# Hybrid decoder trunk on one core: the FFN's weight sums come from accumulating DMAs in DRAM instead of VectorE

## The chip, the cores and the metric

The kernel runs on one core of one Trainium2 chip. The metric is the device time of one execution in microseconds (us). The engines are TensorE (PE), VectorE (DVE), ScalarE (ACT), GpSimd (POOL) and SyncE (SP); DMAs are issued from the queues of SP, ACT or POOL and run on the 16 DMA engines of the core.

## The reference

The model has two layers of width 1024 over 1024 tokens, in float32. Layer 0 mixes by Mamba-2 SSD heads and gMLP heads, layer 1 by a Conformer convolution and HGRN2 heads. Each mixer is followed by a squared-ReLU MLP (FFN), and one RMSNorm ends the model. The part that the change touches is the first half of the MLP:

```python
for layer in range(DEPTH):                      # DEPTH = 2
    ...                                         # mixer: x = x + y
    h = rmsnorm(x, ffn_norm_g[layer])           # x: 1024 x 1024
    x = x + jnp.square(jax.nn.relu(h @ ffn_w1[layer])) @ ffn_w2[layer]   # w1: 1024 x 4096
return rmsnorm(x, final_norm_g)
```

The weights are drawn anew for each set of inputs, so every sum of weights has to be formed on the chip.

## The kernel before

Activations are kept with channels on the 128 partitions and tokens along the free axis, as 8 tiles of 128 x 1024. Every large product is computed in float32 by three matmuls with operands in fp32r: `split` (lines 97 to 100) makes a high part by a cast on ACT and the remainder by a subtraction on DVE, and the matmuls take high x high, high x low and low x high.

The FFN input, `ffn_in`, is one level of Winograd's form of Strassen's product. The 1024 x 1024 input is cut into quadrants (channels in two halves, tokens in two halves). `wino_ops` forms the seven operands of the activation side (B11, B21, T1, T2, T3, B22, T4) while the output projection of the mixer ends, each as a tile whose first 512 columns hold the high part and whose last 512 hold the low part. The 4096 hidden channels are 32 blocks of 128; one *unit* takes two of them, `w1[2u]` and `w1[2u+1]`, each a 128 x 1024 tile in which the columns 0 to 511 are the first half of the input channels and 512 to 1023 the second. There are 16 units in a layer. A unit needs seven products, and a product is 4 x 3 matmuls of 512 columns (lines 330 to 332).

The weight side of the seven products comes from the generator `weights`. It loads two tiles for a unit (`wraw`, three buffers, from SP's queue), forms four sums and differences of quadrants on DVE (`comb`, line 345), and splits all seven operands one by one into tiles of their own: high part in the columns 0 to 511, low part in 512 to 1023. Eight such tiles exist. `nextw` keeps the emission of operands four ahead of the products. The first two products of the first three units (`nhead`) need only plain quadrants and are emitted ahead of the rest; their weight tiles are loaded a second time when the units go on.

After each product the running sums in PSUM are copied by ACT (`snap`), added on DVE, and passed through ReLU and a square on ACT; the hidden tiles go to DRAM from ACT's queue and come back for the FFN output.

The program is written in order, and a scheduler places the instructions of each engine by priority and by its own estimate of when operands are ready; `high_priority` moves a block ahead. `issue_after(ins)` makes the instructions that its block traces on the engine of `ins` queue behind `ins`. Each engine, and each DMA queue, then runs strictly in its own order. SP's queue carries nearly all loads. POOL's carries no DMA in the kernel before, only 12 memsets besides the constants: two on `rmask` at the start (line 1185) and the others for layer 1.

At the start, `gmlp` loads two weight blocks of `wv` in halves of 520 KB and the input x in segments of 256 columns, in turn, on SP's queue, and the first products run as these land. In the SSD part, `prep` reloads a broadcast of the cumulative sums (`A<-acs_d`, 512 KB) for every chunk.

Of the kernel before, what the change touches and what calls it, by code (L numbers as in the profile page):

```python
# [1 line left out]

# [4 lines left out]
F32 = mybir.dt.float32  # L7
# [3 lines left out]
AF = mybir.ActivationFunctionType  # L11
ALU = mybir.AluOpType
# [3 lines left out]
P = 128  # L16
D = 1024
T = 1024
HALF = 512
# [20 lines left out]
HP = 500  # L40
# [4 lines left out]
def R(ap):  # L45
    return ap.bitcast(F32R)
# [10 lines left out]
class Trunk:  # L57
# [178 lines left out]
                self.nc.scalar.activation(rs, rs, AF.Square)  # L236


    def wino_start(self, X, g, spill):
        return dict(X=X, g=g, acc=None, spill=spill, ops={}, late=[])  # L240

    def wino_ops(self, st, r, k):

        nc, X, tt = self.nc, st["X"], self.nc.vector.tensor_tensor
        n = r.stop - r.start

        def op(name, src, q):
            if (name, k) not in st["ops"]:
                st["ops"][name, k] = self.slot(name)
            t = st["ops"][name, k]  # L250
            self.split(src, t[:, q], t[:, HALF + q.start:HALF + q.stop])

        y, z = X[k][:, r], X[k + 4][:, r]
        for i, x in ((k, y), (k + 4, z)):
            nc.scalar.activation(x, x, AF.Copy, scale=self.v(st["g"], i))
        if r.stop <= HALF:
            op("B11", y, r)
            op("B21", z, r)
            return
        q = slice(r.start - HALF, r.stop - HALF)  # L260
        b11, b21 = X[k][:, q], X[k + 4][:, q]
        t2 = self.small([P, n], "bt")
        tt(b11, y, b11, ALU.subtract)
        tt(t2, z, b11, ALU.subtract)
        op("T2", t2, q)
        tt(b21, b21, t2, ALU.subtract)

        def late(name):
            if name == "T3":
                tt(y, z, y, ALU.subtract)  # L270
            op(name, {"T1": b11, "T3": y, "B22": z, "T4": b21}[name], q)

        st["late"].append(late)
# [44 lines left out]
    def ffn_in(self, l, st, hid, load):  # L318

        nc, ops, tt = self.nc, st["ops"], self.nc.vector.tensor_tensor  # L320
        w1, nhead = self.a["w1"][l], self.nhead
        L, H = slice(0, HALF), slice(HALF, 2 * HALF)

        def prod(ps, w, name, first, last):
            for k in range(4):
                b = ops[name, k]
                c = slice(k * P, k * P + P)
                cl = slice(HALF + k * P, HALF + k * P + P)
                mm = nc.tensor.matmul
                mm(ps, R(w[:, c]), R(b[:, L]), start=(first and k == 0), stop=False, skip_group_check=not first)  # L330
                mm(ps, R(w[:, c]), R(b[:, H]), start=False, stop=False, skip_group_check=not first)  # L331
                mm(ps, R(w[:, cl]), R(b[:, L]), start=False, stop=(last and k == 3), skip_group_check=not first)  # L332

        def weights():

            def op(src):
                t = self.wop("wq")
                with self.tc.high_priority(HP):
                    self.split(src, t[:, L], t[:, H])
                return t  # L340

            def comb(x, y, f):
                t = self.small([P, HALF], "ws")
                with self.tc.high_priority(HP):
                    tt(t, x, y, f)
                return t

            raws = lambda u, n: [self.wraw(w1[2 * u + i]) for i in range(n)]
            for u in range(nhead):
                ra, = raws(u, 1)  # L350
                yield op(ra[:, L])
                yield op(ra[:, H])
            for u in range(FF // P // 2):
                ra, rb = raws(u, 2)
                if u >= nhead:
                    yield op(ra[:, L])
                    yield op(ra[:, H])
                S1 = comb(rb[:, L], rb[:, H], ALU.add)
                S2 = comb(S1, ra[:, L], ALU.subtract)
                yield op(S2)  # L360
                yield op(S1)
                yield op(comb(ra[:, L], rb[:, L], ALU.subtract))
                yield op(comb(ra[:, H], S2, ALU.subtract))
                yield op(rb[:, H])

        wq, wsrc = deque(), weights()

        def nextw(ahead=4):
            while len(wq) <= ahead:
                t = next(wsrc, None)  # L370
                if t is None:
                    break
                wq.append(t)
            return wq.popleft()

        def snap(ps):
            t = self.small([P, HALF], "snap")
            with self.tc.high_priority(HP):
                nc.scalar.copy(t, ps)  # L379
            return t  # L380

        def square(t, src=None):
            self.last_relu = nc.scalar.activation(t, t if src is None else src, AF.Relu)
            nc.scalar.activation(t, t, AF.Square)

        def unit(u, ws):
            pa, pb = self.mm_ps(), self.sm_ps()
            prod(pa, ws(), "B11", True, True)
            prod(pb, ws(), "B21", True, True)
            h0 = self.slot("hid")  # L390
            s1 = snap(pa)
            tt(h0[:, L], s1, pb, ALU.add)
            square(h0[:, L])
            yield
            prod(pa, ws(), "T2", False, True)
            s2 = snap(pa)
            pc = self.mm_ps()
            prod(pc, ws(), "T1", True, True)
            s5 = snap(pc)
            prod(pa, ws(), "T3", False, True)  # L400
            s3 = snap(pa)
            h1 = self.slot("hid")
            tt(h1[:, H], s3, s5, ALU.add)
            square(h1[:, H])
            prod(pc, ws(), "B22", False, True)
            tt(h0[:, H], s2, pc, ALU.add)
            square(h0[:, H])
            nc.scalar.dma_start(hid[2 * u], h0)
            prod(pa, ws(), "T4", False, True)
            square(h1[:, L], pa)  # L410
            nc.scalar.dma_start(hid[2 * u + 1], h1)

        units = [unit(u, nextw) for u in range(FF // P // 2)]
        late = lambda *names: [f(name) for name in names for f in st["late"]]
        for u in range(nhead):
            if u == nhead - 2:
                late("T1")
            next(units[u])
        late("T3", "B22", "T4")
        for u, g in enumerate(units):  # L420
            if u == len(units) - 1:
                first = load(0)
            for _ in g:
                pass
            if u == nhead:
                self.lnexp(self.last_relu)
                self.norm_rows(st, True)
        return first

    def ffn(self, l, st, xd, norm_g):  # L430
# [744 lines left out]
    def build(self):  # L1175
        tc, nc, a = self.tc, self.nc, self.a
        with tc.tile_pool(name="kp", bufs=1) as self.kp, tc.tile_pool(name="wp", bufs=1) as self.wp, \
# [18 lines left out]

            st = self.norm_start(X, "mixg0")
            self.gmlp(st)
            X, norm = self.ssd(st, lambda X: self.wino_start(X, "ffng0", self.xd[0]))
            if self.stop == 1:  # L1200
                return self.dump(X)
# [89 lines left out]
```

## Time and profile before

| | |
|---|---|
| median of 3 runs | 2852.56 us (2850.95 to 2855.23) |
| the profiled execution | 2856.86 us, of which its span (first to last instruction) 2855.1 us |
| PE busy | 2815.4 us (99%) |
| DVE busy | 1927.6 us (68%) |
| ACT busy | 1198.3 us (42%) |
| POOL busy | 4.0 us |
| DMA moved | 287.23 MB, mean 101 GB/s |
| chain that ended last | PE 93%, DVE 5%, ACT 1%, DMA 1% |
| FFN input | about 688.7 to 998 us (layer 0), 2174 to 2484 us (layer 1) |

The busy times are of one execution, so they are read against its 2855.1 us and not against the median. Matmuls are pipelined: one of 512 columns is shown with a duration of 393 ns while the next starts some 230 ns after it, so the count of matmuls in a stretch says more of their pace than their durations. "Idle before" and waits are put down to what came last.

### The profile page before, as it was taken

What the parts mean: (1) busy time and instruction counts of PE and PEld (TensorE: products, weight loads), DVE (VectorE), ACT (ScalarE), POOL (GpSimd) and SP (SyncE); (2) the same over time, 40 slices, a digit from 0 to 9 for tenths busy, and PEclk for the clock granted to TensorE, in tenths of its full rate; (3) what the DMA queues carried; (4) which work ended last, traced back from release to release, by engine and by line L of the source; (5) the groups of instructions that cost most, each with busy time, mean ns of one, the idle gap of its engine ahead of it and who ended that gap; (6) DMA issues with size and microseconds to landing.
All of it is one profiled execution on the core that took longest, in us unless ns stands there. A gap on an engine that the chain in (4) does not pass through costs nothing.

```text
span 2855.1 us, 36628 instructions
## 1 busy us (share of the span) xinstructions
PE 2815.4 (99%) x14637; PEld 2361.8 (83%) x14637; DVE 1927.6 (68%) x2985; ACT 1198.3 (42%) x1964; POOL 4.0 (0%) x16
## 2 busy tenths in 40 slices
PE   8999998999999999999999999998999999999998
PEld 8988786778788888889888888888888888888887
DVE  5666878768544566546699998885769544566546
ACT  6421425226655532113534444455347655522112
POOL 0000000000000000000000000000000000000000
PEclk9999999999999999999999999999999999999999
DMA  4131424513333453221211111113313332543211
GB/s 163 45 98 64 140 66 149 188 52 111 118 118 102 150 191 128 86 74 46 102 52 60 63 57 53 53 59 126 139 52 104 133 105 102 175 180 118 85 56 60
DMA packets 100027, 287.23 MB, mean 101 GB/s; under 512 B 10768, under 2 KB 33680, under 8 KB 99856
## 3 DMA queue, kind: packets, MB, share of 16 engines
q1 hardware_dynamic: 83440, 242.47, 26.0%
q10 hardware_dynamic: 16416, 42.42, 3.8%
q8 instruction: 115, 1.88, 0.3%
q14 instruction: 56, 0.46, 0.1%
HBM read 217.61 MB, written 67.24 MB: 100 GB/s over the span
## 4 chain that ended last, share of the span: by engine, by line
PE 93%; DVE 5%; ACT 1%; DMA 1%; issue 1%; SPq 0%; DVEq 0%
PE mm L149 19%; PE mm L151 19%; PE mm L150 19%; PE mm L330 6%; PE mm L331 6%; PE mm L332 6%; PE mm L160 3%; PE mm L161 3%; PE mm L162 3%; DVE cy L900 2%; PE sm L331 1%; PE sm L330 1%; PE sm L332 1%; PE sm L724 1%; PE sm L186 1%
## 5 line engine op out<-in xcount | busy, mean ns | idle before, releaser
L293 DVE TENSOR_TENSOR x<-x,mm 128x512 f32<-128x512 f32 (+1 forms) x416 | 258.8, 623 | 295.3 <-PE mm L151 282.3
L99 ACT CAST wh<-wr 128x1024 fp32r<-128x1024 f32 (+1 forms) x180 | 188.6, 1048 | 567.2 <-PE mm L150 502.3
L149 PE MATMUL mm<-fh,wh 128*128 128x512 f32 (+1 forms) x1152 | 424.9, 369 | 0.0
L151 PE MATMUL mm<-fh,wl 128*128 128x512 f32 (+1 forms) x1152 | 423.6, 368 | 0.0
L150 PE MATMUL mm<-fl,wh 128*128 128x512 f32 (+1 forms) x1152 | 422.4, 367 | 0.0
L149 PE MATMUL mm<-hh,wh 128*128 128x512 f32 x960 | 384.5, 400 | 0.0
L151 PE MATMUL mm<-hh,wl 128*128 128x512 f32 x960 | 379.3, 395 | 0.0
L150 PE MATMUL mm<-hl,wh 128*128 128x512 f32 x960 | 378.5, 394 | 0.0
L900 DVE SCALAR_TENSOR_TENSOR cy<-ag,vec,cy 128x1023 f32<-128x1023 f32 (+14 forms) x240 | 303.8, 1266 | 3.8
L100 DVE TENSOR_TENSOR wl<-wr,wh 128x1024 fp32r<-128x1024 f32 (+1 forms) x180 | 219.9, 1223 | 75.4 <-ACT wh L99 75.1
L151 PEld LDWEIGHTS mm<-fh,wl 128*128 128x128 f32 x1152 | 216.6, 188 | 38.5
L150 PEld LDWEIGHTS mm<-fl,wh 128*128 128x128 f32 x1152 | 216.5, 188 | 38.2
L149 PEld LDWEIGHTS mm<-fh,wh 128*128 128x128 f32 x1152 | 216.9, 188 | 36.9
L160 PE MATMUL mm<-wh,hh 128*128 128x256 f32 (+1 forms) x768 | 219.7, 287 | 9.6 <-ACT hh L225 8.7
L161 PE MATMUL mm<-wl,hh 128*128 128x256 f32 (+1 forms) x768 | 217.4, 284 | 0.8 <-DVE wl L100 0.8
L162 PE MATMUL mm<-wh,hl 128*128 128x256 f32 (+1 forms) x768 | 216.7, 283 | 0.0
L149 PEld LDWEIGHTS mm<-hh,wh 128*128 128x128 f32 x960 | 181.4, 189 | 42.4 <-issue 2.8
L150 PEld LDWEIGHTS mm<-hl,wh 128*128 128x128 f32 x960 | 180.9, 188 | 41.2 <-issue 1.8
L151 PEld LDWEIGHTS mm<-hh,wl 128*128 128x128 f32 x960 | 180.7, 188 | 41.4
L330 PE MATMUL mm<-T,wq 128*128 128x512 f32 x512 | 201.1, 394 | 0.6 <-ACT snap L379 0.6
L331 PE MATMUL mm<-T,wq 128*128 128x512 f32 x512 | 201.2, 394 | 0.0
L332 PE MATMUL mm<-T,wq 128*128 128x512 f32 x512 | 200.6, 394 | 0.0
(299 smaller groups left out, 5055.7 us busy)
## 6 DMA issues: line engine op xcount, KB each, us to landing
wr<-in_w_dram SPq DMA_DIRECT2D x134, 512.0 KB, 3.7
hid<-hid ACTq DMA_DIRECT2D x64, 512.0 KB, 3.6
ft<-hid SPq DMA_DIRECT2D x64, 512.0 KB, 4.8
x<-xd SPq DMA_DIRECT2D x24, 512.0 KB, 10.8
A<-acs_d SPq DMA_DIRECT2D x16, 512.0 KB, 5.9
wr<-in_wig_dram SPq DMA_DIRECT2D x16, 512.0 KB, 3.6
wr<-in_wxbc_dram SPq DMA_DIRECT2D x12, 512.0 KB, 3.6
wr<-in_wv_dram SPq DMA_DIRECT2D x8, 520.0 KB, 6.0
```

The lines of the kernel that those rows point to most:

```text
L100: return self.nc.vector.tensor_tensor(R(lo), t, h, ALU.subtract)
L149: mm(ps, R(wh[:, c]), R(ah[:, r]), start=(first and k == 0), stop=False)
L150: mm(ps, R(wh[:, c]), R(al[:, r]), start=False, stop=False)
L151: mm(ps, R(wl[:, c]), R(ah[:, r]), start=False, stop=(last and k == n - 1))
L160: mm(ps[:, :n], R(ah[:, r]), R(wh[:, c]), start=(k == 0), stop=False)
L161: mm(ps[:, :n], R(ah[:, r]), R(wl[:, c]), start=False, stop=False)
L162: mm(ps[:, :n], R(al[:, r]), R(wh[:, c]), start=False, stop=(k == len(acts) - 1))
L293: nc.vector.tensor_tensor(X[o][:, r], X[o][:, r], ps, ALU.add)
L330: mm(ps, R(w[:, c]), R(b[:, L]), start=(first and k == 0), stop=False, skip_group_check=not first)
L331: mm(ps, R(w[:, c]), R(b[:, H]), start=False, stop=False, skip_group_check=not first)
L332: mm(ps, R(w[:, cl]), R(b[:, L]), start=False, stop=(last and k == 3), skip_group_check=not first)
L900: nc.vector.scalar_tensor_tensor(d, st[:, :T - k], w, d, ALU.mult, ALU.add)
```

## The change

A new function `combine` forms the four weight sums of all 16 units of a layer in a DRAM tile `wc` of 16 x 128 x 2048, by DMAs issued from GpSimd. Per unit the first 1024 columns hold S1 and S2, the last 1024 the two remaining operands, all formed by copies of quadrants and by DMAs that add to what is there (`accum_op`). As only additions are available, the operand S2 has the other sign than before; `wino_ops` forms its activations with the sign that fits (scalar_tensor_tensor in two places), and two of the ReLUs take a scale of -1. `combine` is called for layer 0 after `gmlp` and for layer 1 in the FFN input of layer 0 behind unit 3, each under `issue_after` with an instruction of ACT.

In `ffn_in` the generator loads whole tiles of 1024 columns (two quadrants, or two sums, at a time) and splits them in one cast and one subtraction, so that two operands share a tile of high parts and a tile of low parts. Only the last operand of a unit is loaded with 512 columns. DVE's sums (`comb`) are gone.

```diff
+    def combine(self, w, after):
+        n = w.shape[0] // 2
+        c = self.dp.tile([n, P, 4 * HALF], F32, name=self.nm("wc"))
+        wu = w.rearrange("(u i) p c -> i p u c", i=2)
+        cu = c.rearrange("u p c -> p u c")
+        q = lambda i: slice(i * HALF, i * HALF + HALF)
+        add = dict(accum_op=ALU.add)
+        plan = [(cu[:, :, 1024:2048], wu[0], {}), (cu[:, :, q(0)], wu[1][:, :, q(0)], {}),
+                (cu[:, :, q(1)], wu[0][:, :, q(0)], {}), (cu[:, :, q(2)], wu[1][:, :, q(0)], add),
+                (cu[:, :, q(0)], wu[1][:, :, q(1)], add), (cu[:, :, q(1)], cu[:, :, q(0)], add),
+                (cu[:, :, q(3)], cu[:, :, q(1)], add)]
+        for dst, src, kw in plan:
+            for u in range(0, n, 2):
+                with contextlib.ExitStack() as es:
+                    if after is not None:
+                        es.enter_context(self.tc.issue_after(after.ins))
+                    self.nc.gpsimd.dma_start(dst[:, u:u + 2], src[:, u:u + 2], **kw)
+        return c
...
-        tt(b11, y, b11, ALU.subtract)
-        tt(t2, z, b11, ALU.subtract)
+        neg_sub = lambda o, x, w: nc.vector.scalar_tensor_tensor(o, x, -1.0, w, ALU.mult, ALU.subtract)
+        tt(b11, b11, y, ALU.subtract)
+        neg_sub(t2, b11, z)
         op("T2", t2, q)
-        tt(b21, b21, t2, ALU.subtract)
+        neg_sub(b21, t2, b21)
...
             def op(src):
-                t = self.wop("wq")
+                n = src.shape[1]
+                t, h = self.wraw(src), self.wop("wh")
+                lo = self.wop("wl") if n > HALF else h[:, n:]
                 with self.tc.high_priority(HP):
-                    self.split(src, t[:, L], t[:, H])
-                return t
+                    self.split(t[:, :n], h[:, :n], lo[:, :n])
+                return [(h[:, i:i + HALF], lo[:, i:i + HALF]) for i in range(0, n, HALF)]
...
-                S1 = comb(rb[:, L], rb[:, H], ALU.add)
-                S2 = comb(S1, ra[:, L], ALU.subtract)
-                yield op(S2)
-                yield op(S1)
-                yield op(comb(ra[:, L], rb[:, L], ALU.subtract))
-                yield op(comb(ra[:, H], S2, ALU.subtract))
-                yield op(rb[:, H])
+                    yield from op(w1[2 * u])
+                s1, s2 = op(wc[u][:, 0:1024])
+                yield s2
+                yield s1
+                yield from op(wc[u][:, 1024:2048])
+                yield from op(w1[2 * u + 1][:, HALF:])
...
+                if l == 0:
+                    self.w1c.append(self.combine(self.a["w1"][1], self.last_relu))
...
             self.gmlp(st)
+            self.w1c = [self.combine(a["w1"][0], self.last_gelu)]
```

## Rows read from the trace of the kernel before

**Rows 1.** The page: span, busy time of each engine, chain that ended last.
```profile
span 2855.1 us, 36628 instructions
PE 2815.4 (99%) x14637; PEld 2361.8 (83%) x14637; DVE 1927.6 (68%) x2985; ACT 1198.3 (42%) x1964; POOL 4.0 (0%) x16
...
PE 93%; DVE 5%; ACT 1%; DMA 1%; issue 1%; SPq 0%; DVEq 0%
```

**Rows 2.** Busy time by stage (length; engines; clock, DMA share, GB/s).
```profile
32.00:440.00 408.00, 408.00 (x2274) 346.06 (x2273) 274.65 (x497) 143.68 (x198) 0.00 (x0) 1.00 0.28 87
...
688.70:720.00 31.30, 31.00 (x135) 24.35 (x134) 30.93 (x76) 26.35 (x65) 0.00 (x0) 1.00 0.26 84
720.00:998.00 278.00, 278.00 (x1200) 225.15 (x1201) 137.39 (x220) 163.69 (x286) 1.06 (x2) 1.00 0.36 124
998.00:1300.00 302.00, 302.00 (x1312) 246.35 (x1311) 176.60 (x208) 63.33 (x67) 0.00 (x0) 1.00 0.34 116
```

**Rows 3.** Waits of PE, whole span (total us, times, longest).
```profile
PE mm L160 <- ACT hh L225: 8.7, 2, 8.5
...
PE mm L160 <- ACT wh L99: 0.9, 1, 0.9
PE mm L161 <- DVE wl L100: 0.8, 1, 0.8
PE mm L330 <- ACT snap L379: 0.6, 2, 0.3
```

**Rows 4.** DVE's groups by form (busy us, mean ns | idle before).
```profile
L100 DVE TENSOR_TENSOR wl<-wr,wh 128x1024 fp32r<-128x1024 f32 x172 | 210.0, 1222 | 68.4 <-ACT wh L99 68.2
L100 DVE TENSOR_TENSOR wq<-ws,wq 128x512 fp32r<-128x512 f32 x128 | 80.5, 684 | 2.1 <-ACT wq L99 2.1
...
L345 DVE TENSOR_TENSOR ws<-wr,wr 128x512 f32<-128x512 f32 x32 | 21.9, 684 | 0.0
```

**Rows 5.** Busy time in steps of 4 us at the start.
```profile
4.00:8.00 4.00, 0.00 (x0) 0.00 (x0) 1.41 (x2) 2.14 (x5) 0.00 (x0) 1.00 1.03 377
8.00:12.00 4.00, 3.27 (x11) 2.65 (x12) 2.37 (x4) 3.51 (x9) 0.00 (x0) 1.00 0.98 313
12.00:16.00 4.00, 4.00 (x28) 4.00 (x28) 4.00 (x11) 4.00 (x11) 0.00 (x0) 1.00 0.92 270
16.00:20.00 4.00, 2.32 (x17) 1.90 (x16) 2.74 (x7) 3.32 (x7) 0.00 (x0) 1.00 0.90 321
...
28.00:32.00 4.00, 4.00 (x35) 4.00 (x34) 3.98 (x12) 4.00 (x14) 0.00 (x0) 1.00 0.32 124
```

**Rows 6.** POOL's instructions in order of time (start us, us).
```profile
0.73 0.95 POOL L1185 MEMSET rmask<- 128x1024 bf16 x1 [0.29 <-POOLq L1280]
1.74 0.17 POOL L1186 MEMSET rmask<- 128x16 bf16 x1
983.49 1.13 POOL L1108 MEMSET att<- 128x512 f32 x2 [981.58 <-DVE wq L100]
```

**Rows 7.** The chain that ended last, 0 to 30 us (start us, us).
```profile
11.21 5.98 DMA wr<-in_wv_dram
17.21 1.07 ACT wh L99
```

**Rows 8.** DMA issues (count, KB each, median us to landing).
```profile
A<-acs_d SPq DMA_DIRECT2D x16, 512.0 KB, 5.9
```

**Rows 9.** Waits of DVE, 220 to 440 us.
```profile
DVE A L675 <- DMA A<-acs_d: 2.6, 4, 1.5
```

**Rows 10.** The tile `ug` (ns min/median/max, first and last start).
```profile
L625 ACT ACTIVATE ug<-ug x16: 624/632/636, 127.6 to 210.6; 128x512 f32<-128x512 f32 x16
```

**Rows 11.** DMA of the first 32 us: packets by size, SP's queue.
```profile
DMA packets 6051, 8.44 MB, mean 264 GB/s; under 512 B 800, under 2 KB 5024, under 8 KB 6048
...
q1 hardware_dynamic: 5760, 7.94, 76.2%
```

**Rows 12.** Line 330, matmuls of the T products (first and last start).
```profile
L330 PE MATMUL mm<-T,wq x512: 388/393/505, 705.3 to 2486.6; 128*128 128x512 f32 x171
```

More of the change, by code (lines that the diff above doesn't have):

```diff
@@ L1 @@
+import contextlib
 from collections import deque
@@ L327, in prod @@
                 c = slice(k * P, k * P + P)
-                cl = slice(HALF + k * P, HALF + k * P + P)
                 mm = nc.tensor.matmul
-                mm(ps, R(w[:, c]), R(b[:, L]), start=(first and k == 0), stop=False, skip_group_check=not first)
-                mm(ps, R(w[:, c]), R(b[:, H]), start=False, stop=False, skip_group_check=not first)
-                mm(ps, R(w[:, cl]), R(b[:, L]), start=False, stop=(last and k == 3), skip_group_check=not first)
+                mm(ps, R(w[0][:, c]), R(b[:, L]), start=(first and k == 0), stop=False, skip_group_check=not first)
@@ L334, in weights @@
+                mm(ps, R(w[0][:, c]), R(b[:, H]), start=False, stop=False, skip_group_check=not first)
+                mm(ps, R(w[1][:, c]), R(b[:, L]), start=False, stop=(last and k == 3), skip_group_check=not first)
         def weights():
+            wc = self.w1c[l]
             def op(src):
-                t = self.wop("wq")
+                n = src.shape[1]
+                t, h = self.wraw(src), self.wop("wh")
+                lo = self.wop("wl") if n > HALF else h[:, n:]
                 with self.tc.high_priority(HP):
-                    self.split(src, t[:, L], t[:, H])
@@ L340, in op @@
-                return t
[L342 to L348, printed above, removed]
+                    self.split(t[:, :n], h[:, :n], lo[:, :n])
+                return [(h[:, i:i + HALF], lo[:, i:i + HALF]) for i in range(0, n, HALF)]
             for u in range(nhead):
-                ra, = raws(u, 1)
-                yield op(ra[:, L])
-                yield op(ra[:, H])
+                yield from op(w1[2 * u])
@@ L353, in weights @@
             for u in range(FF // P // 2):
-                ra, rb = raws(u, 2)
                 if u >= nhead:
-                    yield op(ra[:, L])
-                    yield op(ra[:, H])
-                S1 = comb(rb[:, L], rb[:, H], ALU.add)
-                S2 = comb(S1, ra[:, L], ALU.subtract)
-                yield op(S2)
-                yield op(S1)
-                yield op(comb(ra[:, L], rb[:, L], ALU.subtract))
-                yield op(comb(ra[:, H], S2, ALU.subtract))
-                yield op(rb[:, H])
+                    yield from op(w1[2 * u])
@@ L380, in snap, with square @@
             return t
-        def square(t, src=None):
-            self.last_relu = nc.scalar.activation(t, t if src is None else src, AF.Relu)
+        def square(t, src=None, sign=1.0):
+            self.last_relu = nc.scalar.activation(t, t if src is None else src, AF.Relu, scale=sign)
             nc.scalar.activation(t, t, AF.Square)
@@ L403, in unit @@
             tt(h1[:, H], s3, s5, ALU.add)
-            square(h1[:, H])
+            square(h1[:, H], sign=-1.0)
             prod(pc, ws(), "B22", False, True)
@@ L409, in unit @@
             prod(pa, ws(), "T4", False, True)
-            square(h1[:, L], pa)
+            square(h1[:, L], pa, -1.0)
             nc.scalar.dma_start(hid[2 * u + 1], h1)
```

## The prediction, made before the changed kernel had run

> **What bounds the kernel now.** I read first the busy times and the shares of the chain: TensorE (PE) is busy for 2815.4 of 2855.1 us and holds 93% of the chain that ended last [rows 1]. So a change can win only where PE stands still, and those places are few. Next the busy time by stage [rows 2]. The FFN input of layer 0 runs from 688.7 to about 998 us; PE is busy for 31.00 of the first 31.30 us and for all of the 278 us behind. One matmul starts every 278/1200 = 231.7 ns there, and every 302/1312 = 230.2 ns in the FFN output behind it, which the diff doesn't touch. Last the waits of PE [rows 3]: all matmuls of the FFN input together waited 0.6 us, over both layers. The largest entry is the start: 8.7 us, then 0.9 and 0.8 us for the second weight block. VectorE (DVE) is full in the first 31 us of the FFN input (30.93 of 31.30) but at 137/278 = 49% afterwards [rows 2].
>
> **The change part by part.** *Removed.* A unit loses four sums of 512 columns on DVE at 684 ns [rows 4], 2.7 us, and over 32 units 87.6 us. Splits in pairs turn six DVE instructions of 684 ns into three of 1222 ns: 0.44 us a unit, 14 us in all. That is over 100 us of DVE time, and all of it lies beside PE. What PE can get back is bounded by its waits (0.6 us for both layers) and by the pitch: (231.7 - 230.2) ns x 1344 matmuls = 2.0 us a layer, of which the other matmuls in that window explain some. Ends: 0 and -4.6 us; I take -1.2 us, nearer the waits, since these are what DVE or ACT caused. Matmuls, their order and their columns stay.
>
> *Moved and slower.* The operand sums of `wino_ops` become scalar_tensor_tensor with a sign, and the ReLU gets a scale of -1. Their counts stay; 16 to 32 DVE instructions of 256 columns in a layer may each grow by some tens of ns, under 2 us, in the stretch where DVE is full but is also rid of the sums of the first units. I put 0; with that cover gone it would be +2 us, which is in the range.
>
> *Larger tiles.* A first pair is ready for PE only after a cast and a subtraction of 1024 columns, 1222 ns instead of 684 on DVE [rows 4]. The first weights come free one after another while the output projection's last segment runs, so I take 0; bare it would be about 1 us a layer.
>
> *Loads.* A unit now loads 0.52 + 1.05 + 0.26 = 1.84 MB where it loaded 1.05 MB (plus three head tiles twice). 16 units make 29.4 MB for 18.4 MB, 11 MB more in 309 us, 36 GB/s beside the 124 that stand there at a DMA share of 0.36 [rows 2]. That makes about 160, and the engines have moved 377 [rows 5]: 0 us.
>
> *Added: `combine`.* This is the large part. A layer has 16 units; one quadrant over all of them is 16 x 128 x 512 x 4 B = 4.2 MB. The plan copies four (16.8 MB) and accumulates four (16.8 MB); a layer issues 7 x 8 = 56 DMAs, both 112, all on GpSimd's queue (POOL). The trace has no DMA from DRAM to DRAM and none that accumulates. The nearest row is a load at 377 GB/s with the engines full [rows 5]; a copy can hardly take less engine time than a load of its bytes. For an accumulation the near end is 1 load, and with source and old destination both read, 2; the far end I put at 6. At 350 GB/s, of which the kernel's own loads leave about 0.65 (their share is 0.28 from 32 to 440 us [rows 2]), 228 GB/s remain, and the sums of one layer take 16.8 x (1 + f) / 0.228 = 74 x (1 + f) us: 147, 221 or 516 us for f = 1, 2, 6. I take f = 2, nearest to what the work is: 221 us, and both layers 442.
>
> *When it starts* decides the price. `issue_after` orders what its block traces on the engine of the instruction that it is given; that is a ScalarE instruction, and the DMAs are GpSimd's. I read that as no order at all. Their sources are inputs, nothing on their queue makes them wait: POOL is done with its two memsets at 1.9 us and has nothing more until 983 us [rows 6]. So the first copies start at about 2 to 4 us, those of layer 1 right behind or in between, and the engines are full until about 440 us.
>
> *What they hit at the start.* From 4 to 20 us the DMA engines are already full: shares of 1.03, 0.98, 0.92 and 0.90 [rows 5], and PE waits for data. The second weight block is issued at 11.21 us and lands 5.98 us later [rows 7], at 17.2. From 4 us until then 4 x (377 + 313 + 270) + 1.2 x 321 GB/s = 4.2 MB come in, in 13.2 us. With half of the engines' time gone to the copies that takes 26.4 us: +13.2 us. PE then has 48 + 96 matmuls at 4/35 us in hand [rows 5], 16.5 us, and the last 2.1 MB of x need 13 us at half rate, so nothing more is lost. Ends: 0, if the copies get nothing, and +37 (below). I take +13.
>
> *Until 440 us.* Weights are loaded three buffers ahead and bear twice the time. The reloads of `acs_d` don't: 512 KB, median 5.9 us to landing [rows 8], and DVE already waited for four of them [rows 9]. PE itself shows no wait there (408 of 408 us busy [rows 2]), so there is some cover. If each of seven chunks lost the 6 us by which a landing doubles, it would be +42; at full cover 0. I take +4, nearer to the row of PE.
>
> The Trainium skill ("DMA: Bandwidth & Descriptors", section "Anatomy of one DMA") fits a GpSimd-issued DMA as 2.0 us plus its bytes at 436 GB/s; as an estimate by that page, 56 DMAs one after another would take some 190 us a layer, and the sums of both layers end before 400 us. The trace of before has no such DMA to hold against it.
>
> *Sum,* against the profiled execution, 2856.9 us (its span of 2855.1 and 1.8 around it): -1.2 + 13 + 4 = +16, 2872.7 us. That execution lies 4.3 us above the median of the runs (2852.56), so the time I give is 2868 us.
>
> **The rivals.**
> *Not slower.* The copies don't get in the way at the start: their queue gets little of the engines while the loads run, or they do wait for the last GELU, at 210.6 us [rows 10]. Then only the gain is left, 2848 to 2856 us. For it: after 32 us PE never waits for a DMA in this half, and 0.65 of the engines is free. Against it: I see nothing that holds the queue, and the engines are full just in the first 20 us. It decides as soon as the second weight block lands before about 22 us.
> *By packets.* If the engines take turns between queues packet by packet, the size of a packet sets the shares. Of the 6051 packets of the first 32 us, 5024 are under 2 KB [rows 11], most of them x loads with rows of 1 KB; the first copies have rows of 4 KB. Then x gets a fifth, 64 of 320 GB/s: 2.1 MB of x before the second weight block 33 us, and the 2.1 MB of weights at half rate 13 us, 46 for 13.2, +33; then the last x at a third (copies with 2 KB rows) 20 us against 16.5 in hand, +4. With the other terms 2892 us. The Trainium skill says this of the rings of an engine (the same page, "Queues, rings and completion order": round robin, a whole packet from one before the next); whether packets of both sizes count alike no row here shows.
> *Sums too late.* The first sum is wanted by about 705 us [rows 12]. If both layers' passes are mixed in the queue and an accumulation costs f > 3.7, layer 0 ends only at 2 x 74 x (1 + f) > 690 us, and PE waits for it; f = 4.5 gives 814 us, +105, 2970 us. For it: nothing shows what an accumulation costs. Against: 3.7 loads for two reads and a write is much.
> *The reloads of `acs_d`* lose all of 42 us: 2905 us. Against it PE's full stretch.
>
> **How the numbers follow.** Forecast 0.42 (its own range 2859 to 2885), not slower 0.27, by packets 0.18, sums too late 0.08, reloads 0.05. The range of 2850 to 2902 leaves out the late sums, half of the reloads and the faster end of the second case. A measurement of this kernel tells about 0.2% (5.7 us) from no change. Slower: 0.42 + 0.18 + 0.08 + 0.05, less the forecast's low end, 0.72. Of the 0.27, 0.18 are within 0.2%; faster by more, 0.09, needs 5.7 us where I find at most 4.6, so another order of later instructions would have to help. Same with the low end 0.19.
>
> **What would show it.** Right: a GpSimd queue of some 67 MB from about 3 us on, DMA full to beyond 300 us; the second weight block landing near 30 us and PE's waits before 40 us grown from 10 to over 20 us; the FFN input at the same 230 ns a matmul, with DVE far emptier. Wrong: copies that start after 200 us; a first stretch as before; a matmul of the FFN input waiting for a sum; a pitch there below 230 ns, or PE waiting in the FFN input for the larger splits.

## The result, and the profile after

The kernel after takes 2914.75 us (median of 4 runs, 2912.39 to 2921.75), the kernel before 2852.12 us beside it (2850.95 to 2855.23). The ratio is 1.0222 with an interval of [1.0203, 1.0241]: slower by 62.6 us, where +16 had been forecast. The profiled execution took 2921.75 us, 64.9 more than the one before.

The page of the kernel after: span, engines, the copies' queue (packets, MB, share of the 16 engines' time over the span) and the chain.

```profile
span 2919.9 us, 36576 instructions
PE 2831.1 (97%) x14637; PEld 2373.9 (81%) x14637; DVE 1848.9 (63%) x2761; ACT 1189.7 (41%) x1868; POOL 111.1 (4%) x128
...
q0 software_dynamic: 26368, 67.12, 11.4%
...
PE 90%; DMA 5%; DVE 3%; ACT 1%; issue 1%; SPq 0%; DVEq 0%; ACTq 0%
```

Against [rows 1] PE runs as many matmuls, DVE has lost 79 us and the chain has 4% more of DMA. To see where the time went, take two instructions that both kernels have and read when each first starts: the small matmuls of the first norm, behind the start, and the first matmul of the FFN input. First those of before, then those of after (line, count, ns min/median/max, first and last start).

```profile
L564 PE MATMUL sm<-cm,acc x16: 168/250/250, 61.3 to 62.9; 128*128 128x1 f32 x16
L330 PE MATMUL mm<-B,wq x256: 388/392/801, 688.8 to 2483.8; 128*128 128x512 f32 x128
```

```profile
L581 PE MATMUL sm<-cm,acc x16: 168/250/251, 89.6 to 91.2; 128*128 128x1 f32 x16
L354 PE MATMUL mm<-B,wh x256: 387/393/801, 755.9 to 2547.4; 128*128 128x512 f32 x128
```

The start lost 28.3 us (61.3 to 89.6). The stretch between the two marks grew from 627.5 to 666.3 us, +38.8. What lies behind shrank from 2855.1 - 688.8 = 2166.3 to 2164.0 us, -2.3. These three make up the 64.8 us of the span. The edited FFN input is not where the loss is; two earlier places are, in code that the diff leaves alone.

*The start.* POOL's instructions in the kernel after (start us, us), and what moved from 10 to 26 us by queue:

```profile
1.63 0.84 POOL L260 DMA_DIRECT2D wc<-in_w_dram  x1
2.46 0.20 POOL L1203 MEMSET rmask<- 128x16 bf16 x1
2.50 1.39 POOL L260 DMA_DIRECT2D wc<-in_w_dram  x2
12.50 0.69 POOL L260 DMA_DIRECT2D wc<-in_w_dram  x1 [8.62 <-issue]
...
324.25 1.15 POOL L260 DMA_DIRECT2D wc<-wc  x1 [9.14 <-issue]
```

```profile
DMA packets 2072, 5.28 MB, mean 330 GB/s; under 512 B 181, under 2 KB 987, under 8 KB 2072
...
q0 software_dynamic: 1020, 3.92, 76.0%
q1 hardware_dynamic: 1052, 1.36, 27.5%
```

The first copy goes out at 1.63 us. The two queues moved nearly as many packets, 1020 and 1052, but one of the copies' carries 3.92 MB / 1020 = 3.84 KB and one of the loads' 1.29 KB. So the loads that PE waits for got 1.36 of 5.28 MB, 26%. The chain of after shows the consequence, two pieces of x and then the weight block that took 5.98 us in [rows 7]:

```profile
8.47 18.79 DMA x<-in_xT_dram
...
27.28 18.11 DMA wr<-in_wv_dram
...
45.41 1.07 ACT wh L100
```

That block lands at 45.4 us instead of 17.2. PE's two largest waits in the first 100 us (total us, times, longest) stood at 8.7 and 0.9 us in [rows 3]:

```profile
PE mm L161 <- ACT hh L226: 25.2, 7, 13.6
PE mm L161 <- ACT wh L100: 7.8, 1, 7.8
```

*Between the marks.* The chain of after again, in the SSD part, and the landing times of its DMA issues (count, KB, median us), of after and then the second one of before:

```profile
314.55 9.12 DMA A<-acs_d
...
332.31 19.49 DMA A<-acs_d
...
357.22 14.54 DMA A<-acs_d
...
381.14 11.51 DMA A<-acs_d
```

```profile
A<-acs_d SPq DMA_DIRECT2D x16, 512.0 KB, 10.2
...
gt<-gmd SPq DMA_DIRECT2D x8, 512.0 KB, 9.1
```

```profile
gt<-gmd SPq DMA_DIRECT2D x8, 512.0 KB, 4.8
```

`A<-acs_d` took 5.9 us in [rows 8]. The reload `gt<-gmd`, three of which stand in the chain from 526 to 604 us, took 4.8. The reloads of `A` were a small wait of DVE [rows 9] with 408 of 408 us of PE busy up to 440 us [rows 2]; now they stand in the chain. What that does to PE is in the busy times (columns as in [rows 2]), of before and then of after between the marks and in one hole of 2-us steps:

```profile
61.30:688.80 627.50, 619.84 (x3264) 511.60 (x3263) 444.01 (x800) 229.21 (x307) 0.00 (x0) 0.99 0.32 103
```

```profile
89.60:755.90 666.30, 632.41 (x3264) 519.28 (x3263) 443.72 (x798) 228.00 (x304) 88.32 (x86) 0.97 0.71 172
...
346.00:348.00 2.00, 2.00 (x12) 1.66 (x11) 0.00 (x0) 0.00 (x0) 0.55 (x1) 1.00 1.02 295
...
350.00:352.00 2.00, 0.00 (x0) 0.00 (x0) 0.18 (x1) 0.00 (x0) 0.00 (x0) 0.95 1.07 330
352.00:354.00 2.00, 0.00 (x0) 0.00 (x0) 2.00 (x8) 0.00 (x0) 0.68 (x1) 0.50 0.97 294
...
360.00:362.00 2.00, 2.00 (x15) 1.57 (x13) 1.97 (x3) 1.11 (x2) 0.69 (x1) 0.50 1.00 389
...
366.00:368.00 2.00, 2.00 (x10) 1.62 (x10) 0.00 (x0) 0.00 (x0) 0.10 (x1) 1.00 1.01 274
```

The same 3264 matmuls: idle time grew from 7.7 to 33.9 us (+26.2), busy time by 12.6 us. The mean granted clock fell from 0.99 to 0.97, and the hole shows how: PE ran out of work while the reload of 332.31 us took 19.49 us to land, the granted clock went from 1.00 to 0.50 (from 2.4 to 1.2 GHz) in the idle steps, was still 0.50 from 360 to 362 us with PE full again, and was back at 1.00 from 366 us. Busy time x (1 - granted clock), summed over the stretch in steps of 1 us, is 17.2 us in after and 5.6 in before, so the lower clock accounts for 11.6 of the 12.6 us of busy time. A wait for a DMA thus cost more than its own length, here by some four tenths (11.6 on 26.2).

*The FFN input* itself, layer 0 of after, 67.1 us later than [rows 2]:

```profile
787.10:1065.10 278.00, 278.00 (x1202) 225.47 (x1201) 97.69 (x113) 157.50 (x240) 0.99 (x2) 1.00 0.47 160
```

1202 matmuls where there were 1200, a pitch of 231.3 for 231.7 ns, and DVE at 97.69 for 137.39 us: 40 us of DVE's work went and PE's pace stayed.

### The profile page after: what moved, and what is told of

Its sections match the earlier page's. It is cut to its first block, busy times and chain, and to the rows that moved or that the text cites. A ratio compares the mean times of both kernels' runs of the same rounds, so it can differ in the third digit from the quotient of the medians.

```text
span 2919.9 us, 36576 instructions
## 1 busy us (share of the span) xinstructions
PE 2831.1 (97%) x14637; PEld 2373.9 (81%) x14637; DVE 1848.9 (63%) x2761; ACT 1189.7 (41%) x1868; POOL 111.1 (4%) x128
## 3 DMA queue, kind: packets, MB, share of 16 engines
q0 software_dynamic: 26368, 67.12, 11.4%
## 4 chain that ended last, share of the span: by engine, by line
PE 90%; DMA 5%; DVE 3%; ACT 1%; issue 1%; SPq 0%; DVEq 0%; ACTq 0%
PE mm L150 18%; PE mm L151 18%; PE mm L152 18%; PE mm L354 6%; PE mm L356 6%; PE mm L355 6%; PE mm L161 3%; PE mm L162 3%; PE mm L163 3%; DMA A<-acs_d 2%; PE sm L354 1%; PE sm L356 1%; PE sm L355 1%; DMA gt<-gmd 1%; DMA x<-in_xT_dram 1%; DMA wr<-in_wv_dram 1%
## 5 line engine op out<-in xcount | busy, mean ns | idle before, releaser
L101 DVE TENSOR_TENSOR wl<-wr,wh 128x1024 fp32r<-128x1024 f32 (+1 forms) x276 | 337.5, 1223 | 360.9 <-issue 203.3
L100 ACT CAST wh<-wr 128x1024 fp32r<-128x1024 f32 (+2 forms) x308 | 308.8, 1003 | 613.7 <-PE mm L151 510.2
L354 PE MATMUL mm<-T,wh 128*128 128x512 f32 x512 | 201.7, 394 | 0.0
L355 PE MATMUL mm<-T,wh 128*128 128x512 f32 x512 | 200.6, 392 | 0.0
L161 PEld LDWEIGHTS mm<-wh,hh 128*128 128x128 f32 x768 | 147.4, 192 | 37.0 <-ACT hh L226 27.0
```

Source lines behind the costliest of these rows:

```text
L100: self.nc.scalar.copy(R(h), t)
L101: return self.nc.vector.tensor_tensor(R(lo), t, h, ALU.subtract)
L161: mm(ps[:, :n], R(ah[:, r]), R(wh[:, c]), start=(k == 0), stop=False)
L354: mm(ps, R(w[0][:, c]), R(b[:, L]), start=(first and k == 0), stop=False, skip_group_check=not first)
L355: mm(ps, R(w[0][:, c]), R(b[:, H]), start=False, stop=False, skip_group_check=not first)
```

## The experiments

Each run is read by the same three stretches. Kernels with "gate" share a helper that makes GpSimd itself wait; it gives the `combine` of after an instruction on the engine that issues its DMAs:

```diff
+    def pool_gate(self, src):
+        g = self.kp.tile([P, 16], F32, tag=self.nm("pg"), bufs=1, name=self.nm("pg"))
+        self.nc.scalar.copy(g, src)
+        return self.nc.gpsimd.memset(g, 0.0)
```

| run | to the norm's matmuls | from there to the FFN input | behind | ratio to before |
|---|---|---|---|---|
| before | 61.3 | 627.5 | 2166.3 | |
| after | 89.6 | 666.3 | 2164.0 | 1.0222 [1.0203, 1.0241] |
| e1, no sums | 59.4 | 627.5 | 2162.2 | 0.9994 [0.9985, 1.0004] |
| e2, layer 1's sums in the FFN input | 89.3 | 626.8 | 2169.9 | 1.0116 [1.0101, 1.0131] |
| e3, both gated, from 69 and 786 us | 60.2 | 632.2 | 2169.5 | 1.0019 [1.0010, 1.0029] |
| e4, both gated, from 218 and 786 us | 59.6 | 637.5 | 2166.2 | 1.0041 [1.0026, 1.0056] |
| e5, first pass in 1 KB rows | 62.6 | 651.9 | 2164.5 | 1.0102 [1.0085, 1.0119] |
| e6, ring of twice the size | 102.8 | 640.4 | 2162.8 | one run, 2907.86 us |
| e7, copies in place of additions | 87.7 | 626.0 | 2162.4 | 1.0094 [1.0079, 1.0109] |
| e8, gated, layer 1 in the FFN output | 59.3 | 628.3 | 2176.2 | 1.0060 [1.0042, 1.0077] |
| e9, gated, layer 1 in the output projection | 60.4 | 644.9 | 2168.6 | 1.0104 [1.0087, 1.0121] |
| e10, 1 KB rows and twice the ring | 92.1 | 648.8 | 2162.5 | one run, 2905.22 us |

**e1: the rest of the change without the sums.** `Plain` hands out tiles of w1 itself where the sums stood, in both layers.

```diff
-            self.w1c = [self.combine(a["w1"][0], self.last_gelu)]
+            self.w1c = [Plain(a["w1"][0])]
```

> Leaves out the weight sums: no combine at all; FFN input loads w1's own tiles of the same size in the place of the sums. Theory A (all of the loss is the DMA traffic of combine, in two places: the copies at the start and the reloads of the SSD part): 2851 us, between 2847 and 2855, FFN input at 230 ns a matmul, PE waits before 40 us back at about 10 us. Rival B (pairs of 1024 columns, 11 MB more loads a layer, or another order of instructions cost part of it): over 2858 us. Rival C (DVE relief pays in the FFN input): under 2847 us.

Measured: 2850.85 us, the ratio's interval holds 1. Both losses are gone, so they belong to the DMAs of `combine` and to nothing else in the diff. Behind the FFN's first matmul the stretch is 4.1 us shorter than before; over the runs without copies or sums there (after, e1, e5, e6, e7, e10) it is 1.8 to 4.1 us shorter. By these single executions that is all that the lighter FFN input gives, over two layers.

**e2, e3, e4: moving the sums in time.** Layer 1's `combine` behind the FFN input's norm (e2), layer 0's also behind the first norm's row factors (e3) or behind the last GELU, as the call in the diff names it (e4).

```diff
-                    self.w1c.append(self.combine(self.a["w1"][1], self.last_relu))
+                    self.w1c.append(self.combine(self.a["w1"][1], self.pool_gate(st["acc"][:, 0:16])))
...
+                self.w1c = [self.combine(a["w1"][0], self.pool_gate(self.rows[:, 0:16]))]
...
-            self.w1c = [self.combine(a["w1"][0], self.last_gelu)]
```

> Layer 0's sums as in the change, from 2 us; layer 1's held on POOL until the FFN input of layer 0. Theory A: the start's loss stays (PE idle before 100 us about 33 us, +23 to +27), the loss between 324 and 680 us goes but for the tail of layer 0's accumulations: 2880 us, 2872 to 2890; nothing lost in the FFN stages. Rival B (the engines' total time is the price, wherever it falls): 2900 us or more, with new PE waits behind 770 us. Rival D (the mid loss comes from layer 0's passes too, or from the order of instructions): stays over 2900 us with waits for A between 324 and 680 us.

> Layer 0's sums held on POOL until the row factors of the first norm (about 65 us), layer 1's until the FFN input of layer 0. Theory A: the start is as before (PE waits about 10 us in the first 100 us); layer 0's passes last some 320 us, to about 390, and meet the reloads of A from 285 us on: +5 to +15, 2857 to 2867 us. Rival B: still +40 or more.

> As the names in the change say, but with a true wait: layer 0's sums behind the last GELU (about 211 us), layer 1's in the FFN input of layer 0. Theory A: start as before; copies from 211 to 285 us, accumulations to about 530 us, over all reloads of A and gt: worse than with the wait at 65 us, 2865 to 2885 us. Rival B: +40 or more. Rival E (the scheduler's order for ACT's table loads or the reloads changes most): no relation to when the passes run.

Measured: 2886.29, 2858.65 and 2864.82 us. e2 keeps the start's loss (+28.0) and has none between the marks (-0.7): the +38.8 comes from layer 1's passes alone, which in after run from 325 to 674 us over the reloads. Layer 0's passes, over by about 320 us in e2, end before these begin to matter. e3 removes the start's loss by starting the copies at 69 us, and is left 6.0 us above before. e4, in which layer 0's sums run from 218 to 559 us, pays +10.0 between the marks. e2 also loses 3.6 us behind the FFN input's first matmul, where nothing was expected; e4's time lies just under its expected range, e3's in it.

How many of the sums lie over the SSD part is not what decides: e4's cover about as much of it as layer 1's do in after, and cost a quarter. The difference is in the first reloads of `A`. Busy times of the same 785 matmuls, from the issue of the first reload to that of the eighth on the list of issues, in before, after and e4 (columns as in [rows 2]), and the time of layer 1's copies in after:

```profile
284.70:435.13 150.43, 150.43 (x785) 120.23 (x784) 118.49 (x218) 54.23 (x61) 0.00 (x0) 1.00 0.36 110
```

```profile
313.10:486.61 173.51, 157.19 (x785) 124.26 (x784) 118.30 (x218) 53.51 (x61) 30.31 (x36) 0.94 0.84 227
...
325.00:409.00 84.00, 68.63 (x355) 53.33 (x354) 47.18 (x107) 24.96 (x29) 16.94 (x25) 0.88 0.97 297
```

```profile
283.13:435.52 152.39, 150.56 (x785) 120.26 (x784) 118.00 (x218) 53.66 (x61) 20.66 (x18) 1.00 0.79 176
```

After loses 23.1 of its 38.8 us here, e4 2.0. In e4 the last copy goes out at 282 us, so nearly all that lies over these reloads is accumulations; up to 371 us the reloads land in 9.4 us (median), the longest in 9.9. In after layer 1's copies go out from 325 to 402 us, the engines are full, and the landings reach 19.5 us. Landings of twice the time were nearly covered; those of three times were not. Full engines do it without copies too: in e10 (below) accumulations at twice the pace hold the DMA share at 1.10 from 321 to 360 us, one landing takes 19.1 us, and the same 785 matmuls lose 16.7 us.

**e5: the packet rival by itself.** The first pass is cut into four of 256 columns.

```diff
-        plan = [(cu[:, :, 1024:2048], wu[0], {}), (cu[:, :, q(0)], wu[1][:, :, q(0)], {}),
+        plan = [(cu[:, :, 1024 + i:1280 + i], wu[0][:, :, i:i + 256], {}) for i in range(0, 1024, 256)]
+        plan += [(cu[:, :, q(0)], wu[1][:, :, q(0)], {}),
...
```

> The change with its first pass of copies cut into four passes of 256 columns, so that their rows have 1 KB, as the x loads, instead of 4 KB. By packets (the engines take one packet of each queue in turn): the x loads get half of the bytes instead of a quarter, the second weight block lands at about 32 us instead of 45.4, the norm's small matmuls start at 73 to 80 us instead of 89.6; 2915 becomes 2897 to 2907 us. By equal shares of time or bytes (my forecast before the result): start as in the change, 2910 us or more.

Measured: 2881.86 us, the norm's matmuls at 62.6 us, far better than either theory said. But the DMA view from 10 to 26 us shows that the edit did something else than was meant:

```profile
q1 hardware_dynamic: 3291, 3.88, 68.1%
q0 software_dynamic: 659, 2.17, 37.2%
```

A packet of the copies is still 2.17 MB / 659 = 3.3 KB, though a row is 1 KB now. There are fewer of them: each of POOL's DMAs holds 0.26 MB instead of 1.05, it had issued three by 4 us and then went on one at a time (8.27, 9.75, 11.17, 14.31 us). By the counts (659 to 3291) the queue was often empty between them. That suggests that what it keeps ready decides its share, and that size had not been in either theory.

**e6, e10: that size by itself.** The space for the descriptors of GpSimd's DMAs is doubled, in after (e6) and in e5 (e10). For room, a pool of tiles goes from 14 to 12 buffers.

```diff
-    nc = _bacc.Bacc("TRN2", target_bir_lowering=False, num_devices=1, dynamic_dma_scratch_size=1024)
+    nc = _bacc.Bacc("TRN2", target_bir_lowering=False, num_devices=1, dynamic_dma_scratch_size=2048)
```

> The change with a descriptor ring of 2048 bytes a partition for GpSimd's DMAs instead of 1024 (and 12 instead of 14 small work tiles, to make room). If the ring limits the accumulations, they follow each other faster than every 7 us and both layers' sums end well before 600 us instead of 680 us. If each accumulation is bound by itself, the interval stays at 7 to 9 us. The start's loss stays about 28 us in both cases.

> First pass with rows of 1 KB, and the ring of 2048 bytes. If what counts at the start is how many bytes of copies stand ready in the ring (64 rows of 1 KB an engine emptied before POOL refilled it, 64 rows of 4 KB did not), twice the ring lets the copies take more of the packets again: between 10 and 26 us more than 1200 of their packets for the 659 of the run with the small ring, and the norm's small matmuls start at 66 to 85 us instead of 62.6. If the row size itself decides, they stay at 62 to 65 us with about 660 packets.

Measured: the norm's matmuls at 102.8 us in e6, where both theories had less loss, and at 92.1 in e10 against 62.6 with the same rows and half the space (66 to 85 had been expected, and over 1200 packets of the copies where 1126 came). The DMA view from 10 to 26 us, e6 and then e10:

```profile
q0 software_dynamic: 1038, 3.99, 77.2%
q1 hardware_dynamic: 1037, 1.35, 26.6%
```

```profile
q0 software_dynamic: 1126, 3.69, 67.7%
q1 hardware_dynamic: 1602, 1.75, 33.7%
```

In e6 the two queues took 1038 and 1037 packets, as if one each in turn, and kept to it: from 42 to 50 us it was 625 and 620, where after had 408 and 1019. In e10 the doubled space brings the loss back that the cut pass had removed. Each is one run, and none takes the smaller pool of tiles by itself, but the shifts of 13.2 and 29.5 us stand against 59.3 to 61.3 us in the six kernels without a loss at the start. How many DMAs stand ready shows in POOL's first issues, here of e6:

```profile
1.63 0.84 POOL L266 DMA_DIRECT2D wc<-in_w_dram  x1
...
2.50 4.07 POOL L266 DMA_DIRECT2D wc<-in_w_dram  x6
12.06 0.70 POOL L266 DMA_DIRECT2D wc<-in_w_dram  x1 [5.49 <-issue]
```

Seven go out at once where after had three. It is also three in e5 and seven in e10, though a DMA there has a quarter of the bytes. All of these have 256 rows, so neither bytes nor packets fill the space; rows or DMAs do.

The other half of e6 is the pace of the accumulations. POOL's issues in after, then in e6:

```profile
140.35 1.14 POOL L260 DMA_DIRECT2D wc<-in_w_dram  x1 [5.90 <-issue]
149.30 1.14 POOL L260 DMA_DIRECT2D wc<-in_w_dram  x1 [7.81 <-issue]
156.13 1.16 POOL L260 DMA_DIRECT2D wc<-in_w_dram  x1 [5.69 <-issue]
```

```profile
139.25 1.14 POOL L266 DMA_DIRECT2D wc<-wc  x1 [3.69 <-issue]
142.99 1.14 POOL L266 DMA_DIRECT2D wc<-wc  x1 [2.60 <-issue]
145.51 1.15 POOL L266 DMA_DIRECT2D wc<-wc  x1 [1.38 <-issue]
```

Over layer 0's 32 accumulations that is one every 8.0 us on average (78 to 324 us) against one every 3.6 (64 to 175 us); the last one of both layers goes out at 347 us, and the loss between the marks falls from 38.8 to 12.9 us. Of these, 10.9 fall ahead of the first reload of `A`, a place where after lost 0.1: there two small loads of gMLP, `bs` and `wsr`, stand in e6's chain and land in 11.1 and 10.4 us (2.4 and 2.8 in before). In after an accumulation lands in 8.7 us (median), so one or two were in flight.

**e7: are the additions what makes the sums long?**

```diff
-        add = dict(accum_op=ALU.add)
+        add = {}
```

> Leaves out the additions: all passes of combine are plain copies of the same bytes. If the length of the accumulations carries the traffic into the SSD part: both layers' passes end by about 300 us, the start's loss stays (28 us), the loss between the first norm and the FFN input (38.8 us) falls under 8: 2876 to 2890 us. If the bytes alone do it: over 2900 us.

Measured: 2880.19 us. All passes end by 295 us, the stretch between the marks is 1.5 us shorter than before, and `A<-acs_d` lands in 6.2 us; the start's loss stays (+26.4). The queue of the copies over the whole run:

```profile
q0 software_dynamic: 18176, 67.12, 7.1%
```

67.12 MB of copies take 7.1% of 2876.1 us, 3.04 us of all engines a MB. In after half of the bytes are such copies and the queue has 11.4% of 2919.9 us, which leaves 6.9 us a MB for the half that accumulates: 2.3 copies.

**e8, e9: a place where the traffic costs nothing?** Layer 0 as in e3; layer 1's sums behind the first chunk of the FFN output (e8), or behind the last split of the SSD's output projection (e9).

```diff
+            if c == 0 and len(self.w1c) == 1:
+                self.w1c.append(self.combine(self.a["w1"][1], self.pool_gate(X[7][:, 1008:1024])))
```

> Both layers' sums where no engine waits for a DMA: layer 0's behind the row factors (65 us), layer 1's behind the first chunk of layer 0's FFN output (about 1036 us, after the reload of x). Theory A: the 3.2 us that the run with layer 1's sums in the FFN input lost behind it go, 4 to 5 us before the FFN input stay: 2852 to 2857 us. Not below 2849 us, since without any combine it is 2851 us. Rival: the sums meet the loads of the FFN output or of layer 1's start, 2860 us or more.

> Layer 0's sums behind the row factors (65 us) as before; layer 1's behind the last split of the SSD output (about 630 us), so that they run beside the output projection and the FFN input of layer 0 and end at about 960 us, before x is reloaded at 1004 us. Theory A: no reload that an engine waits for lies under either stretch; the FFN input starts within 2 us of 688.8, and the time is that of the kernel before or of the run without any sums: 2849 to 2856 us, no gain over 0.2%. Rival (DMA traffic of 34 MB a layer always costs some us wherever it runs): 2858 us or more, as the two runs with layer 1's sums in the FFN stages.

Measured: 2868.86 us (its runs spread from 2863 to 2881) and 2881.91 us; in both theory A failed and the rival held. The stretches are those of the profiled executions, 2865.58 and 2875.70 us, so they hold less than the whole loss. In e8 nothing is lost before the FFN input, and +9.9 us behind it. Its chain shows the hidden tiles that come back for the FFN output:

```profile
1047.69 12.38 DMA ft<-hid
...
1065.79 11.78 DMA ft<-hid
```

From 1040 to 1360 us they land in 8.0 us (median), against 4.8 over the whole run of before. In e9 the spill of x, `xd<-x`, lands in 5.7 us instead of 2.0, PE waits 11.7 us from 600 to 760 us for the additions that read its products (0 in before), and the FFN input starts 16.5 us later than before. Each of these stretches has a reload or spill that only looked covered. No version beats the kernel before; without any sums (e1) the time is 1.8 us lower, too little to tell from none.

## Why the prediction was right in its direction and wrong in its size

*Right.* The copies start at once (1.63 us; 2 to 4 was said), since an ordering behind a ScalarE instruction does not hold GpSimd's queue. 67.12 MB go through that queue. The FFN input gains next to nothing: -1.2 us was taken from PE's waits and the pitch with an end of -4.6; behind its first matmul the runs show -1.8 to -4.1. No product waited for a sum, and the FFN input's loads moved at 160 GB/s as worked out. DVE's busy time fell by 79 us, not by the over 100 worked out from mean durations, and that bought nothing because PE had not waited for it.

*Wrong, the first step: "With half of the engines' time gone to the copies that takes 26.4 us: +13.2 us".* The start cost +28.3, all of it in this term: the second weight block landed 28.2 us later. The shares are not halves: the two queues moved as many packets each (1020 to 1052; 1038 to 1037), and a packet of the copies is three times as large. This is the prediction's rival "by packets", with x at a fifth and +37; measured were 26% and +28.3. The Trainium skill ("DMA: Bandwidth & Descriptors", section "Queues, rings and completion order") says that each DMA engine goes round the queues that have work, one packet from each; the trace agrees with that by these counts. What the rival lacked is how much the copies' queue keeps ready, which e5, e6 and e10 move the loss by, from 1.3 to 41.5 us.

*Wrong, the second step: "I take +4, nearer to the row of PE".* Measured +38.8. That this lies near the step's far end of 42 is luck: the 42 was seven doubled landings up to 440 us, and the runs show something else. Doubled landings were nearly covered (e4, 2.0 us over the first eight reloads). What the step lacked is landings of up to 19.5 us, beside layer 1's copies, 23.1 us over the same reloads; the loss behind 440 us, as the sums ran until 674 us instead of 442; and the lower clock after each hole, 11.6 us of the whole. Layer 1's copies fell on the reloads because layer 0's accumulations ahead of them were slow (in e6 and e7, where these copies are over earlier, the same 785 matmuls lose 2.9 and 0.0 us). Their price in engine time was nearly right (f = 2 was taken; 2.3 measured), but they did not run at the engines' rate: one or two accumulations stood in flight, 8.0 us apart on average (e6, e7). With f = 2.3 at the assumed rate both layers would have ended at 2 x 74 x 3.3 = 488 us. The Trainium skill's fit for one such DMA (the same page, "Anatomy of one DMA") had given an estimate of 190 us a layer; layer 0's last is issued at 324 us, so the measurement decides against it.

*Wrong in the chances.* The two rivals at the start and at the reloads were priced as alternatives, 2892 and 2905 us, each with its chance, and the range ended between them. They are two places of one traffic, and both happened: 2856.9 - 2.3 + 28.3 + 38.8 = 2921.7.

*Left open.* Whether rows or DMAs fill the descriptor space no run separates. Why 10.9 us of e6's loss fall on `bs` and `wsr` is told from landings alone. e9's loss is told from landings and waits, and no run takes the spill away.

## What to carry to other kernels

Work that goes to idle DMA engines to relieve an engine that nobody waits for can only cost: look first at what PE waits for, then at each load on the way to PE and ask what twice its landing time does. A stretch in which PE is always busy does not tell how much longer its loads may take: here twice the landing time was nearly covered and three times was not, so keep the engines from being full while such loads run. Prefetches on another queue need an order on the engine that issues them, and two harms that one traffic does at two places are added, not weighed against each other.

## What the runs showed of the hardware

- Two DMA queues moved as many packets each while the packets of one were three times as large: 1038 to 1037 in 16 us, 3.99 to 1.35 MB (e6).
- Copies with rows of 1 KB moved in packets of 3.3 KB on average, so shorter rows did not make small packets (e5).
- Three DMAs of 256 rows went out from GpSimd at once, whether of 1 MB or of 256 KB, and seven with twice the descriptor space.
- Twice the descriptor space of GpSimd's DMAs halved the interval of its accumulations (8.0 us down to 3.6 on average) and cost the start another 13 us.
- An accumulation from DRAM to DRAM took 6.9 us of all 16 engines a MB, a copy 3.04; the 64 accumulations moved in 8192 packets more than the same bytes as copies (26368 to 18176).
- Reloads of 512 KB landed in 6.1 us (median) in before (285 to 364 us), 9.4 beside accumulations (at most 9.9, e4), and up to 19.5 beside copies that filled the engines.
- After a hole of 8.1 us in PE's work (348.7 to 356.8 us) the granted clock stood at 0.50, and matmuls ran at it before it was 1.00 again; over the stretch the lower clock cost 17.2 us beside 33.9 us of idle time (5.6 beside 7.7 in before).
